# A decoder layer on one Trainium2 core: the second RMSNorm's last squares and powers moved forward, and the first weight splits of the MLP held behind named instructions

## The chip, the cores and the metric

The kernel runs on one core of one Trainium2 chip. The metric is device time in microseconds, the median of three runs of the whole program. A core has a matrix engine (TensorE, in the rows PE, with its weight loads as PEld), a vector engine (VectorE, DVE), an activation engine (ScalarE, ACT), a general engine (GpSimd, POOL) and an engine that issues most of the loads (SyncE, SP). Each works through its own instructions in a fixed order, and they wait for each other by semaphores.

## The reference, cut to what matters

One layer over 256 tokens of width 1024, everything in float32. Three attention mixers and their gates come first and are not touched here. What the change touches is the seam between the end of that part and the gated MLP:

```
x = x + merged @ w_out
h = rmsnorm(x, norm_ffn)                  # x * rsqrt(mean(x*x) + 1e-6) * g, row by row
u = h @ w_up                              # 1024 -> 2 * 2816
u = causal depthwise conv of width 3 over the tokens, + bias
x = x + (silu(u[:, :2816]) * u[:, 2816:]) @ w_down
out = rmsnorm(x, norm_final)
```

## The kernel before

**Products in three parts.** Every float32 operand of a matmul is split into a rounded high part (`hi`, written by ScalarE as fp32r) and the remainder (`lo`, by VectorE). `mm3` then makes three products: lo by hi, hi by lo, hi by hi. A weight unit (`Unit`) is 128 x 2048 numbers, loaded by one DMA of SyncE into a `raw` tile; ScalarE writes `whi` from it in two halves (L223) and VectorE writes `wlo = raw - whi` in two halves (L227). Five units are in flight at a time.

**The middle.** Tokens are in two tiles of 128 (t = 0, 1), channels in two halves of 512 (n = 0, 1). Four sums `acc[t][n]` in PSUM hold the output projection. As each is finished (`flush`), VectorE adds the residual into `xs` (L750, `add(t, n)`), ScalarE squares it and sums the row (L168, `square(t, n)`), and TensorE turns it into channel-major order (L760, `turned`). ScalarE scales the turned blocks by g and writes `hn_hi` (L767), VectorE writes `hn_lo` from the turned block in PSUM and `hn_hi` in SBUF (L770).

**The norm is applied late.** The MLP's first products (unit `fa0`, the first 256 columns of the activated half, and `fu0`, of the other half, into four PSUM tiles `firsts`) are made with x * g, not yet divided by the root mean square. The factor is made on the side: VectorE adds the two half sums of squares and epsilon (`msf`, L177), GpSimd raises them to the power -0.5 (`rsf`, L179), two matmuls against the identity spread them over all partitions (L822), ScalarE copies that to SBUF (`rows`, L823), and VectorE multiplies each product by it (L841 in `conv`).

**Order.** From the first `flush` to the end of the first products, the code says the order on all engines but SyncE (`manual_schedule`). A scheduler places what comes after that (the further units, `fd0`, `fd1`, `fa2`, ...), and may put it between those instructions. On TensorE the middle is: turn, 16 products with `hn_hi` (the first four of eight blocks k), turn, 16 with `hn_lo`, 16 with `hn_hi` (the other four k), 16 with `hn_lo`, the two spreading matmuls, 32 products with `wlo` (L827). Then come the MLP's units: per 128 channels c, 24 products for each half, the convolution (one ScalarE pass L842 and two VectorE passes L844), silu (L861), the product (L863), its split into `fh` (L866) and `fl` (L867), and, one channel block later, 12 products of 512 columns into the output sums (`later`). `fd0` is the first unit of w_down, needed for the first of these.

Of the kernel before, what the change touches and what calls it, by code (L numbers as in the profile page):

```python
# [127 lines left out]
def decoder_layer(ctx: ExitStack, tc, x, small_b, table, w1, wts, norms, out):  # L128
# [77 lines left out]
    class Unit:  # L206
# [17 lines left out]

        def lo(self, i, steps, eng=None):
            sl = slice(self.size * i // steps, self.size * (i + 1) // steps)
            (eng or nc.vector).tensor_sub(self.parts[1][:, sl], self.raw[:, sl], self.parts[0][:, sl].bitcast(F32))  # L227

        def split(self, steps, eng):
            for i in range(steps):  # L230
# [521 lines left out]
    def square(t, n):  # L752
        return square_mean(xs[:, t, HALF[n]], spare[0][:, HALF[n]], f"f{t}{n}")
# [15 lines left out]
    def turn_lo(c):  # L769
        nc.vector.scalar_tensor_tensor(h_lo[:, c, :], xT[c], g_ffn[:, c:c + 1], h_hi[:, c, :].bitcast(F32),  # L770
                                       op0=ALU.mult, op1=ALU.subtract)

    fu = dict(first)
    firsts = [gtile() for _ in range(4)]

    def first_products(part, b, ks):

        for k in ks:
            for i in range(2):
                for j, u in enumerate((fu["fa0"], fu["fu0"])):  # L780
                    nc.tensor.matmul(firsts[2 * i + j], u[part][:, k, i * P:(i + 1) * P], b[:, k, :],
                                     start=b is h_hi and k == 0, stop=False)

    with tc.manual_schedule(engines={mybir.EngineType.Activation, mybir.EngineType.DVE, mybir.EngineType.Pool,
                                     mybir.EngineType.PE}):

        sq = {}
        for t in range(NT):
            flush(t, 0)
            add(t, 0)  # L790
            sq[t, 0] = square(t, 0)
        flush(0, 1)
        add(0, 1)
        xT += turned(0)
        flush(1, 1)

        def split_x(c0):

            for c in (c0, c0 + 1):
                turn_hi(c)  # L800
            for c in (c0, c0 + 1):
                turn_lo(c)
        split_x(0)
        add(1, 1)
        split_x(2)
        first_products(0, h_hi, range(4))
        u_f.lo(0, 2)
        xT += turned(1)
        first_products(0, h_lo, range(4))
        split_x(4)  # L810
        split_x(6)
        first_products(0, h_hi, range(4, KC))
        u_f.lo(1, 2)
        for t in range(NT):
            sq[t, 1] = square(t, 1)
        rs = [rstd_of([sq[t, 0], sq[t, 1]], f"f{t}") for t in range(NT)]
        fu["fa1"] = unit("fa1")
        first_products(0, h_lo, range(4, KC))

        rp = psa.tile([P, 512], F32, name="acc00")[:, :S]  # L820
        for t in range(NT):
            nc.tensor.matmul(rp[:, t * P:(t + 1) * P], rs[t].to_broadcast([P, P]), ident, start=True, stop=True)  # L822
        nc.scalar.activation(rows, rp, AF.Copy)  # L823
        for i in range(4):
            for k in range(KC):
                u = fu[("fa0", "fu0")[i % 2]]
                nc.tensor.matmul(firsts[i], u[1][:, k, i // 2 * P:(i // 2 + 1) * P], h_hi[:, k, :], start=False,  # L827
                                 stop=k == KC - 1)
        fu["fu1"] = unit("fu1")
    waiting.clear()  # L830


    merge.close()
    mpool = ctx.enter_context(tc.tile_pool(name="ffn", bufs=2))
    acc = sums()

    def conv(ps, ch):
        y = mpool.tile([P, S], F32, name="cy", bufs=3)
        u = scaled.pop(0)
        scaled.append(u)  # L840
        nc.vector.tensor_mul(u, ps, rows)  # L841
        nc.scalar.activation(y, u, AF.Identity, bias=vec_c[:, 3, ch:ch + 1], scale=vec_c[:, 2, ch:ch + 1])  # L842
        for w, sh in ((1, 1), (0, 2)):
            nc.vector.scalar_tensor_tensor(y[:, sh:], u[:, :S - sh], vec_c[:, w, ch:ch + 1], y[:, sh:],  # L844
                                           op0=ALU.mult, op1=ALU.add)
        return y

    for i in range(NFF // 2):
        ua, uu, ud = (fu.pop(f"f{w}{i}", None) or unit(f"f{w}{i}", 4 if i == 1 and w != "d" else 2) for w in "aud")
        for c in range(2):  # L850
            ch = 2 * i + c

            def up(u):
                ps = gtile()
                for k in range(KC):
                    mm3(ps, u[0][:, k, c * P:(c + 1) * P], u[1][:, k, c * P:(c + 1) * P],
                        h_hi[:, k, :], h_lo[:, k, :], k == 0, k == KC - 1)
                return ps
            a = conv(firsts[2 * ch] if ch < 2 else up(ua), ch)
            sa = mpool.tile([P, S], F32, name="sa")  # L860
            nc.scalar.activation(sa, a, AF.Silu)  # L861
            b = conv(firsts[2 * ch + 1] if ch < 2 else up(uu), NFF + ch)
            nc.vector.tensor_mul(sa, sa, b)  # L863
            fh = mpool.tile([P, S], F32R, name="fh", bufs=4)
            fl = mpool.tile([P, S], F32R, name="fl", bufs=4)
            nc.scalar.activation(fh, sa, AF.Copy)  # L866
            nc.vector.tensor_sub(fl, sa, fh.bitcast(F32))  # L867
            later(acc, fh, fl, ud, c, ch == 0, ch == NFF - 1, 1 if ch < NFF - 3 else 3)
# [39 lines left out]
```

## Time and profile before

| what | value |
|---|---|
| median of 3 runs | 440.69 us (439.71 to 441.37) |
| the profiled execution | 441.25 us |
| its span, first to last instruction | 439.4 us |
| mean granted TensorE clock, as a share of full speed | 0.991 |
| TensorE busy | 428.6 us, 98% of the span |
| VectorE busy | 307.0 us, 70% |
| ScalarE busy | 241.6 us, 55% |
| GpSimd busy | 16.3 us, 4% |
| loads from HBM | 76.52 MB |

The profiled execution lasts 1.85 us longer than its span, and 0.56 us longer than the median. Busy matmul time is modelled at its ends, so the starts of matmuls say more than their busy time. An engine that is off the path has idle time that costs nothing; what counts is where TensorE, the busiest one, stands still or runs at a lower clock.

### The profile page before, as it was taken

The numbers are of one execution on the slowest core, as the hardware profiler recorded it, in microseconds if no ns is written. First come the engines' busy times: TensorE is split into PE (matmuls) and PEld (weight loads), VectorE is DVE, ScalarE is ACT, GpSimd is POOL, SyncE is SP. The second block draws the span as 40 slices with busy tenths as digits, with TensorE's granted clock in tenths as the row PEclk, the third lists the DMA queues.
The fourth block names the chain that finished last, engine by engine and source line by source line (L and its number), as shares of the span: only waits on it lengthen the run. The fifth ranks groups of instructions, "written<-read, shape, count | busy, mean of one in ns | idle before, by whom it ended". The sixth has DMA issues, their size and how long they took to land.

```text
span 439.4 us, 7725 instructions
## 1 busy us (share of the span) xinstructions
PE 428.6 (98%) x3104; PEld 392.2 (89%) x3104; DVE 307.0 (70%) x637; ACT 241.6 (55%) x421; POOL 16.3 (4%) x19
## 2 busy tenths in 40 slices
PE   8999999999999999999999899999999999999993
PEld 8998877976789998999998799999999999999982
DVE  5666743888465597549355789897797887887854
ACT  6443452458676774455346686465465564574423
POOL 4201000000000000000000300000000000000001
PEclk9999999999999999999999999999999999999998
DMA  8989545431027694544540455752752733700002
GB/s 307 393 321 355 204 157 227 169 119 68 31 101 272 273 367 187 192 151 154 204 164 0 172 213 198 280 205 99 271 188 101 288 147 142 285 3 1 2 0 95
DMA packets 12611, 78.09 MB, mean 178 GB/s; under 512 B 1392, under 2 KB 1408, under 8 KB 4640
## 3 DMA queue, kind: packets, MB, share of 16 engines
q1 hardware_dynamic: 12000, 75.48, 46.2%
q0 software_dynamic: 576, 2.12, 1.5%
q8 instruction: 24, 0.39, 0.4%
q14 instruction: 11, 0.09, 0.1%
HBM read 76.52 MB, written 1.07 MB: 177 GB/s over the span
## 4 chain that ended last, share of the span: by engine, by line
PE 91%; DVE 2%; issue 2%; POOL 2%; DMA 1%; ACT 1%; POOLq 0%; SPq 0%
PE g L241 21%; PE g L239 21%; PE g L240 21%; PE acc L239 6%; PE acc L240 6%; PE acc L241 6%; PE s L443 3%; PE o L475 2%; PE t L454 2%; DMA raw<-in_wts_dram 1%; PE g L827 1%; PE o L537 1%; POOL rsf L179 1%; POOL wlo L227 1%; DVE hn_lo L770 1%
## 5 line engine op out<-in xcount | busy, mean ns | idle before, releaser
L227 DVE TENSOR_TENSOR wlo<-raw,whi 128x1024 fp32r<-128x1024 f32 (+2 forms) x130 | 152.8, 1206 | 51.5 <-ACT whi L223 51.1
L239 PE MATMUL g<-hn_hi,wlo 128*128 128x256 f32 x632 | 180.7, 286 | 0.0
L241 PE MATMUL g<-hn_hi,whi 128*128 128x256 f32 x632 | 179.9, 285 | 0.0
L240 PE MATMUL g<-hn_lo,whi 128*128 128x256 f32 x632 | 179.9, 285 | 0.0
L223 ACT ACTIVATE whi<-raw 128x1024 fp32r<-128x1024 f32 (+2 forms) x130 | 129.6, 1039 | 40.8 <-PE g L241 28.4
L239 PEld LDWEIGHTS g<-hn_hi,wlo 128*128 128x128 f32 x632 | 121.1, 192 | 3.8 <-issue 2.3
L240 PEld LDWEIGHTS g<-hn_lo,whi 128*128 128x128 f32 x632 | 121.1, 192 | 2.7 <-issue 1.9
L241 PEld LDWEIGHTS g<-hn_hi,whi 128*128 128x128 f32 x632 | 121.1, 192 | 1.4 <-issue 1.3
L844 DVE SCALAR_TENSOR_TENSOR cy<-xn,small_b,cy 128x255 f32<-128x255 f32 (+1 forms) x88 | 41.8, 481 | 11.4 <-ACT cy L842 10.4
L842 ACT ACTIVATE cy<-xn,small_b 128x256 f32<-128x256 f32 x44 | 26.0, 596 | 17.2 <-DVE xn L841 17.2
L239 PE MATMUL acc<-whi,fl 128*128 128x512 f32 x88 | 34.5, 392 | 0.0
L240 PE MATMUL acc<-wlo,fh 128*128 128x512 f32 x88 | 34.5, 392 | 0.0
L241 PE MATMUL acc<-whi,fh 128*128 128x512 f32 x88 | 34.2, 389 | 0.0
L866 ACT ACTIVATE fh<-sa 128x256 fp32r<-128x256 f32 x22 | 9.1, 416 | 33.8 <-DVE sa L863 33.8
L841 DVE TENSOR_TENSOR xn<-g,xn 128x256 f32<-128x256 f32 x44 | 18.5, 422 | 13.2 <-PE g L241 9.6
L654 ACT ACTIVATE gl<-g 128x256 f32<-128x256 f32 x24 | 9.1, 381 | 23.9 <-PE g L241 23.9
L241 PEld LDWEIGHTS acc<-whi,fh 128*128 128x128 f32 x88 | 16.5, 188 | 3.6
L239 PEld LDWEIGHTS acc<-whi,fl 128*128 128x128 f32 x88 | 16.6, 189 | 3.0
L240 PEld LDWEIGHTS acc<-wlo,fh 128*128 128x128 f32 x88 | 16.6, 189 | 2.8
L240 PE MATMUL g<-o_lo,whi 128*128 128x256 f32 x64 | 18.1, 283 | 0.0
L241 PE MATMUL g<-o_hi,whi 128*128 128x256 f32 x64 | 18.1, 283 | 0.0
L239 PE MATMUL g<-o_hi,wlo 128*128 128x256 f32 x64 | 18.1, 283 | 0.0
(180 smaller groups left out, 512.9 us busy)
## 6 DMA issues: line engine op xcount, KB each, us to landing
raw<-in_wts_dram SPq DMA_DIRECT2D x62, 1024.0 KB, 4.9
gl<-in_w_dram SPq DMA_DIRECT2D x8, 512.0 KB, 7.3
raw<-in_wts_dram SPq DMA_DIRECT2D x2, 804.0 KB, 7.8
raw<-in_wts_dram SPq DMA_DIRECT2D x3, 512.0 KB, 6.4
T<-tvd POOLq DMA_DIRECT2D x1, 1280.0 KB, 13.2
xs<-in_x_dram SPq DMA_DIRECT2D x2, 516.0 KB, 3.7
out_dram<-raw SPq DMA_DIRECT2D x4, 256.0 KB, 2.2
T<-tvd POOLq DMA_DIRECT2D x1, 768.0 KB, 8.4
```

The lines of the kernel that those rows point to most:

```text
L223: nc.scalar.activation(self.parts[0][:, sl], self.raw[:, sl], AF.Copy)
L227: (eng or nc.vector).tensor_sub(self.parts[1][:, sl], self.raw[:, sl], self.parts[0][:, sl].bitcast(F32))
L239: nc.tensor.matmul(ps, al, bh, start=start, stop=False)
L240: nc.tensor.matmul(ps, ah, bl, start=False, stop=False)
L241: nc.tensor.matmul(ps, ah, bh, start=False, stop=stop)
L443: nc.tensor.matmul(pss[i][:, o], q[rows, q0:q0 + P], k[rows, 0:k1], start=True, stop=True)
L454: nc.tensor.transpose(ps[:, i * P:(i + 1) * P], b, ident)
L654: nc.scalar.activation(gl[c][:, b, :], chunk_T(plain(u, c)), AF.Copy)
L841: nc.vector.tensor_mul(u, ps, rows)
L842: nc.scalar.activation(y, u, AF.Identity, bias=vec_c[:, 3, ch:ch + 1], scale=vec_c[:, 2, ch:ch + 1])
L844: nc.vector.scalar_tensor_tensor(y[:, sh:], u[:, :S - sh], vec_c[:, w, ch:ch + 1], y[:, sh:], op0=ALU.mult, op1=ALU.add)
L866: nc.scalar.activation(fh, sa, AF.Copy)
```

## The change

It reorders the middle and touches no arithmetic. The squares of the second channel half move on ScalarE in front of the second four `hn_hi` blocks, and their `msf` on VectorE behind the fourth `hn_lo` block; the two spreading matmuls move in front of the last 16 `hn_lo` products. The two `lo` halves of `fu0` now stand together behind all eight `hn_lo`. `fa1` and `fu1` are split at places that the code names, `fd0` is held until `rows` and the second `lo` half of `fu1` are done (`issue_after`, which tells the scheduler behind which instruction it may place the work), and the units of the next two channel pairs behind a convolution's ScalarE pass each. The multiplication by `rows` becomes `by_rstd`, called where the product ends.

```diff
         split_x(0)
         add(1, 1)
         split_x(2)
+        for t in range(NT):
+            sq[t, 1] = square(t, 1)
         first_products(0, h_hi, range(4))
-        u_f.lo(0, 2)
+
+        rs = [rstd_of([sq[t, 0], sq[t, 1]], f"f{t}") for t in range(NT)]
         xT += turned(1)
         first_products(0, h_lo, range(4))
         split_x(4)
         split_x(6)
+        for i in range(2):
+            u_f.lo(i, 2)
+        u_n = Unit("fa1")
+        fu["fa1"] = u_n.views
+        for i in range(2):
+            u_n.hi(i, 2)
         first_products(0, h_hi, range(4, KC))
-        u_f.lo(1, 2)
-        for t in range(NT):
-            sq[t, 1] = square(t, 1)
-        rs = [rstd_of([sq[t, 0], sq[t, 1]], f"f{t}") for t in range(NT)]
-        fu["fa1"] = unit("fa1")
-        first_products(0, h_lo, range(4, KC))
 
         rp = psa.tile([P, 512], F32, name="acc00")[:, :S]
         for t in range(NT):
             nc.tensor.matmul(rp[:, t * P:(t + 1) * P], rs[t].to_broadcast([P, P]), ident, start=True, stop=True)
-        nc.scalar.activation(rows, rp, AF.Copy)
+        on_act = [nc.scalar.activation(rows, rp, AF.Copy)]
+        for i in range(2):
+            u_n.lo(i, 2)
+        first_products(0, h_lo, range(4, KC))
+        u_n = Unit("fu1")
+        fu["fu1"] = u_n.views
+        for i in range(2):
+            u_n.hi(i, 2)
         for i in range(4):
             for k in range(KC):
                 u = fu[("fa0", "fu0")[i % 2]]
                 nc.tensor.matmul(firsts[i], u[1][:, k, i // 2 * P:(i // 2 + 1) * P], h_hi[:, k, :], start=False,
                                  stop=k == KC - 1)
-        fu["fu1"] = unit("fu1")
+            if i < 3:
+                firsts[i] = by_rstd(firsts[i])
+            if i < 2:
+                on_dve = u_n.lo(i, 2)
     waiting.clear()
+    with tc.issue_after(on_act[0].ins), tc.issue_after(on_dve.ins):
+        fu["fd0"] = unit("fd0")
...
     for i in range(NFF // 2):
-        ua, uu, ud = (fu.pop(f"f{w}{i}", None) or unit(f"f{w}{i}", 4 if i == 1 and w != "d" else 2) for w in "aud")
+        with tc.issue_after(on_act[3 + i].ins) if i in (1, 2) else ExitStack():
+            ua, uu, ud = [fu.pop(f"f{w}{i}", None) or unit(f"f{w}{i}") for w in "aud"]
```

On TensorE, before, behind the second turning (L760): `rsf` is the power, `g` the four `firsts`, the tile after the last `acc` is the spread factor.

```order
L781 MATMUL g<-hn_hi,whi 128x256 x16
L760 MATMUL acc_2853<-ident,xs 128x128 x4
L760 MATMUL acc_2854<-ident,xs 128x128 x4
L781 MATMUL g<-hn_lo,whi 128x256 x16
L781 MATMUL g<-hn_hi,whi 128x256 x16
L781 MATMUL g<-hn_lo,whi 128x256 x16
L822 MATMUL acc_2940<-ident,rsf_2910 128x128
L822 MATMUL acc_2940<-ident,rsf_2914 128x128
L827 MATMUL g<-hn_hi,wlo 128x256 x32
```

The same place on TensorE in the changed kernel (L787, L831 and L843 are the old L781, L822 and L827):

```order
L787 MATMUL g<-hn_hi,whi 128x256 x16
L760 MATMUL acc_2864<-ident,xs 128x128 x4
L760 MATMUL acc_2865<-ident,xs 128x128 x4
L787 MATMUL g<-hn_lo,whi 128x256 x16
L787 MATMUL g<-hn_hi,whi 128x256 x16
L831 MATMUL acc_2922<-ident,rsf_2858 128x128
L831 MATMUL acc_2922<-ident,rsf_2862 128x128
L787 MATMUL g<-hn_lo,whi 128x256 x16
L843 MATMUL g<-hn_hi,wlo 128x256 x32
```

The two spreading matmuls have moved ahead of 16 products; no row has come or gone.

On VectorE, before, from the residual addition of the last quarter on (`msf` is the mean of squares, `wlo` the lo half of a weight unit, `xn` a product times `rows`):

```order
L750 TENSOR_TENSOR xs<-acc_1949,xs 128x512
L770 SCALAR_TENSOR_TENSOR hn_lo<-acc_2812,xs,hn_hi 128x256 x2
L227 TENSOR_TENSOR wlo<-raw,whi 128x1024 x2
L770 SCALAR_TENSOR_TENSOR hn_lo<-acc_2853,xs,hn_hi 128x256 x2
L770 SCALAR_TENSOR_TENSOR hn_lo<-acc_2854,xs,hn_hi 128x256 x2
L227 TENSOR_TENSOR wlo<-raw,whi 128x1024
L177 TENSOR_SCALAR msf_2908<-ssf_2793,ssf_2904 128x1
L177 TENSOR_SCALAR msf_2912<-ssf_2802,ssf_2906 128x1
L227 TENSOR_TENSOR wlo<-raw,whi 128x1024 x3
L841 TENSOR_TENSOR xn_2779<-g,xn_2779 128x256
L227 TENSOR_TENSOR wlo<-raw,whi 128x1024 x2
```

And in the changed kernel (L776 is the old L841):

```order
L750 TENSOR_TENSOR xs<-acc_1949,xs 128x512
L770 SCALAR_TENSOR_TENSOR hn_lo<-acc_2812,xs,hn_hi 128x256 x2
L177 TENSOR_SCALAR msf_2856<-ssf_2793,ssf_2836 128x1
L177 TENSOR_SCALAR msf_2860<-ssf_2802,ssf_2838 128x1
L770 SCALAR_TENSOR_TENSOR hn_lo<-acc_2864,xs,hn_hi 128x256 x2
L770 SCALAR_TENSOR_TENSOR hn_lo<-acc_2865,xs,hn_hi 128x256 x2
L227 TENSOR_TENSOR wlo<-raw,whi 128x1024 x4
L776 TENSOR_TENSOR xn_2779<-g,xn_2779 128x256
L227 TENSOR_TENSOR wlo<-raw,whi 128x1024
L776 TENSOR_TENSOR xn_2779<-g,xn_2779 128x256
L227 TENSOR_TENSOR wlo<-raw,whi 128x1024
```

The two `msf` stand three weight halves earlier, right in front of four `hn_lo`; behind them four weight halves are in one row.

On ScalarE, before, from the first four `hn_hi` to `rows` (L823); `ssf` are the sums of squares:

```order
L767 ACTIVATE hn_hi<-acc_2811,xs 128x256 x2
L767 ACTIVATE hn_hi<-acc_2812,xs 128x256 x2
L223 ACTIVATE whi<-raw 128x1024 x2
L767 ACTIVATE hn_hi<-acc_2853,xs 128x256 x2
L767 ACTIVATE hn_hi<-acc_2854,xs 128x256 x2
L168 ACTIVATE xn_2778,ssf_2904<-xs 128x512
L168 ACTIVATE xn_2778,ssf_2906<-xs 128x512
L223 ACTIVATE whi<-raw 128x1024 x3
L823 ACTIVATE xn_2779<-acc_2940 128x256
L223 ACTIVATE whi<-raw 128x1024 x2
```

And in the changed kernel (L832 is the old L823, L860 the old L842):

```order
L767 ACTIVATE hn_hi<-acc_2811,xs 128x256 x2
L767 ACTIVATE hn_hi<-acc_2812,xs 128x256 x2
L168 ACTIVATE xn_2778,ssf_2836<-xs 128x512
L168 ACTIVATE xn_2778,ssf_2838<-xs 128x512
L767 ACTIVATE hn_hi<-acc_2864,xs 128x256 x2
L767 ACTIVATE hn_hi<-acc_2865,xs 128x256 x2
L223 ACTIVATE whi<-raw 128x1024 x2
L832 ACTIVATE xn_2779<-acc_2922 128x256
L223 ACTIVATE whi<-raw 128x1024 x4
L860 ACTIVATE cy<-xn_2779,small_b 128x256 x3
```

The squares stand in the place of two halves of a weight unit (`fd0`), and these come behind `rows`.

## Rows read from the trace of the kernel before

**Rows 1.** Page: busy time, share of the span and instructions of each engine.
```profile
PE 428.6 (98%) x3104; PEld 392.2 (89%) x3104; DVE 307.0 (70%) x637; ACT 241.6 (55%) x421; POOL 16.3 (4%) x19
```

**Rows 2.** Chain that ended last, 246 to 257 us: start, us, what.
```profile
246.74 3.87 POOL rsf L179
```

**Rows 3.** Timeline of TensorE: start, us to the last end, line, tiles, count [idle before].
```profile
241.80 1.04 PE L760 MATMUL acc<-ident,xs 128*128 128x128 f32 x8
242.59 2.15 PE L781 MATMUL g<-hn_lo,whi 128*128 128x256 f32 x16
244.58 2.08 PE L781 MATMUL g<-hn_hi,whi 128*128 128x256 f32 x16
246.50 2.08 PE L781 MATMUL g<-hn_lo,whi 128*128 128x256 f32 x16
250.65 1.32 PE L822 MATMUL acc<-ident,rsf 128*128 128x128 f32 x4 [2.07 <-POOL rsf L179]
256.74 0.28 PE L239 MATMUL g<-hn_hi,wlo 128*128 128x256 f32 x1
...
263.34 0.40 PE L239 MATMUL acc<-whi,fl 128*128 128x512 f32 x1
...
282.22 0.40 PE L239 MATMUL acc<-whi,fl 128*128 128x512 f32 x1
```

**Rows 4.** Stretches around the wait: busy time of engines, granted clock, DMA share, GB/s.
```profile
251.00:254.40 3.40, 3.39 (x17) 3.22 (x16) 0.61 (x2) 2.39 (x4) 0.13 (x1) 0.50 1.00 410
254.40:256.70 2.30, 2.30 (x21) 2.30 (x21) 2.30 (x3) 2.30 (x3) 0.00 (x0) 1.00 0.61 246
```

**Rows 5.** Timeline of GpSimd, beginning, middle and end of the program.
```profile
8.81 4.77 POOL L227 TENSOR_TENSOR wlo<-raw,whi 128x1024 fp32r<-128x1024 f32 x2 [1.06 <-ACT whi L306]
...
246.74 4.39 POOL L179 TENSOR_TENSOR rsf<-msf,half 128x1 f32<-128x1 f32 x2 [211.66 <-DVE msf L177]
...
430.09 0.93 POOL L179 TENSOR_TENSOR rsz<-msz,half 128x1 f32<-128x1 f32 x1 [178.96 <-DVE msz L177]
```

**Rows 6.** Timeline of VectorE beside these GpSimd instructions.
```profile
10.80 1.65 DVE L315 SCALAR_TENSOR_TENSOR hn_lo<-t,xs,hn_hi 128x256 fp32r<-128x256 f32 x4
...
246.69 3.50 DVE L227 TENSOR_TENSOR wlo<-raw,whi 128x1024 fp32r<-128x1024 f32 x3
...
429.93 0.68 DVE L877 TENSOR_TENSOR raw<-xs,g 128x512 f32<-128x512 f32 x1
```

**Rows 7.** Timeline of ScalarE: the squares, the `hn_hi` and the silu table.
```profile
238.27 1.57 ACT L767 ACTIVATE hn_hi<-acc,xs 128x256 fp32r<-128x256 f32 x4 [0.30 <-PE acc L760]
...
242.43 1.57 ACT L767 ACTIVATE hn_hi<-acc,xs 128x256 fp32r<-128x256 f32 x4 [0.34 <-PE acc L760]
243.88 0.65 ACT L168 ACTIVATE xn<-xs 128x512 f32<-128x512 f32 x1
244.65 0.63 ACT L168 ACTIVATE xn<-xs 128x512 f32<-128x512 f32 x1
...
257.86 1.28 ACT L861 ACT_TABLE_LOAD   x1
```

**Rows 8.** Timeline of VectorE in the middle and the MLP's first channels.
```profile
240.08 0.69 DVE L750 TENSOR_TENSOR xs<-acc,xs 128x512 f32<-128x512 f32 x1
240.69 0.87 DVE L770 SCALAR_TENSOR_TENSOR hn_lo<-acc,xs,hn_hi 128x256 fp32r<-128x256 f32 x2
...
243.74 1.66 DVE L770 SCALAR_TENSOR_TENSOR hn_lo<-acc,xs,hn_hi 128x256 fp32r<-128x256 f32 x4
...
253.79 0.42 DVE L841 TENSOR_TENSOR xn<-g,xn 128x256 f32<-128x256 f32 x1 [3.61 <-PE g L827]
...
264.19 0.75 DVE L841 TENSOR_TENSOR xn<-g,xn 128x256 f32<-128x256 f32 x2
...
281.04 0.41 DVE L867 TENSOR_TENSOR fl<-sa,fh 128x256 fp32r<-128x256 f32 x1
```

**Rows 9.** Stretch 240.69 to 281.46 us: busy PE, PEld, DVE, ACT, POOL (instructions), clock, DMA, GB/s.
```profile
240.69:281.46 40.77, 38.69 (x277) 36.81 (x276) 35.85 (x62) 27.34 (x43) 4.39 (x2) 0.96 0.59 214
```

More of the change, by code (lines that the diff above doesn't have):

```diff
@@ L226, in lo @@
             sl = slice(self.size * i // steps, self.size * (i + 1) // steps)
-            (eng or nc.vector).tensor_sub(self.parts[1][:, sl], self.raw[:, sl], self.parts[0][:, sl].bitcast(F32))
+            return (eng or nc.vector).tensor_sub(self.parts[1][:, sl], self.raw[:, sl], self.parts[0][:, sl].bitcast(F32))
         def split(self, steps, eng):
@@ L771, in turn_lo, with by_rstd @@
                                        op0=ALU.mult, op1=ALU.subtract)
+    def by_rstd(ps):
+        u = scaled.pop(0)
+        scaled.append(u)
+        nc.vector.tensor_mul(u, ps, rows)
+        return u
     fu = dict(first)
@@ L835, in decoder_layer, with conv @@
     acc = sums()
-    def conv(ps, ch):
+    def conv(u, ch):
         y = mpool.tile([P, S], F32, name="cy", bufs=3)
[L839 to L842, printed above, removed]
+        on_act.append(nc.scalar.activation(y, u, AF.Identity, bias=vec_c[:, 3, ch:ch + 1], scale=vec_c[:, 2, ch:ch + 1]))
         for w, sh in ((1, 1), (0, 2)):
@@ L857, in up @@
                         h_hi[:, k, :], h_lo[:, k, :], k == 0, k == KC - 1)
-                return ps
+                return by_rstd(ps)
             a = conv(firsts[2 * ch] if ch < 2 else up(ua), ch)
@@ L861, in decoder_layer @@
             nc.scalar.activation(sa, a, AF.Silu)
-            b = conv(firsts[2 * ch + 1] if ch < 2 else up(uu), NFF + ch)
+            b = conv(firsts[1] if ch == 0 else by_rstd(firsts[3]) if ch == 1 else up(uu), NFF + ch)
             nc.vector.tensor_mul(sa, sa, b)
```

## The prediction

> **What bounds the kernel now.** I read the page first: TensorE is busy for 98% of the span [rows 1], so a change can only pay where TensorE stands or runs slow. The chain of work that ended last shows the one long piece in it that isn't TensorE's: the first power on GpSimd, 3.87 us from 246.74 [rows 2]. TensorE's timeline shows what that costs [rows 3]. Products of 256 columns start 0.12 us apart when nothing is in the way (16 of them from 244.58 to 246.50). The last 16 `hn_lo` products start at 246.50, so the spreading matmuls could start at 248.42; they start at 250.65, after an idle time that ends with the power. The first MLP product starts at 256.74.
>
> The table of stretches shows a second loss [rows 4]: from 251.00 to 254.40 the granted clock is 0.50, that is 1.2 GHz in place of 2.4, behind an idle time of 2.07 us; from 254.40 on it is 1.00 again. The mean from 240.69 to 281.46 is 0.96 [rows 9], which these 3.4 us account for (1.7 of 40.77), so there is no other fall nearby. 3.4 us at half speed do 1.7 us of work.
>
> Why is the power slow? It begins at 246.74 and the pair of powers takes 4.39 us [rows 5], so the second takes about 0.52: a power by itself is short. VectorE runs three `wlo` subtractions from 246.69 to 250.19 [rows 6], and the first power ends 0.42 us after them (246.74 + 3.87 = 250.61). At the end of the program a power begins at 430.09, under a VectorE product of two SBUF operands that runs from 429.93 to 430.61, and ends at 431.02, 0.41 us after it. Two cases, one pattern: the power gets through only when the VectorE subtraction or product is over, and a run without a gap holds it for the whole run. The opposite case is there too: while GpSimd subtracted `wlo` from 8.81 to 13.58 [rows 5], VectorE's `hn_lo` form, whose first operand is in PSUM, took 1.65 us for four [rows 6], as in the middle, where GpSimd was idle (1.66) [rows 8]. That form doesn't collide.
>
> **The change, part by part.** *Powers.* ScalarE ends its first four `hn_hi` at 239.84 (238.27 + 1.57), and squares follow each other by 0.77 us [rows 7]. The first moved square runs from 239.84 to 240.6; the second needs the last residual addition, which ends at 240.77 [rows 8], and ends at about 241.55. VectorE is through its fourth `hn_lo` at 241.56, makes `msf` and then has nothing to do until the next `hn_hi` pair is there, at 242.43 + 0.8 = 243.25 [rows 7]. So the powers run from about 241.75, 0.5 each, to 242.85. Even without that pause the four `hn_lo` that follow don't hold them; the first subtraction of SBUF operands comes behind these, at 243.25 + 1.66 = 244.9. The powers have 3.15 us for 1.1. TensorE asks for them at 246.50.
>
> The Trainium skill ("SBUF — State Buffer", Who interferes with whom) gives this its rule: a VectorE instruction with two SBUF inputs and a GpSimd instruction that reads SBUF exclude each other for a whole instruction, and one with at most one SBUF input doesn't contend. The trace agrees with the second half (1.65 against 1.66 us, above); of the first half it shows more than the rule says, a hold over three instructions.
>
> *TensorE.* From 246.50 to 256.74 it now spends 10.24 us. The same instructions without wait and at full clock: 48 products of 0.12 are 5.76, and the four records of the spreading matmuls at the pace of the eight turning matmuls (241.80 to 242.59, 0.10 each) are 0.40; together 6.16. **Gain 4.08 us**, the MLP starting at 252.66. It is made of 2.23 of waiting (250.65 less 248.42) and 1.85 of slow clock and of the second power (6.09 us from 250.65 to 256.74, against 4.24). The wait alone, with the clock still falling, is the lower bound, 2.2; if the spreading matmuls keep the 0.33 us each that their row allows (1.32 / 4), the gain is 3.2. I take 4.08: nothing stands in front of them to cool the engine.
>
> *What moves on ScalarE.* The squares go in front of the second four `hn_hi`, which wait for the turning until 242.43 anyway; the squares are done at 241.55. Cover 0.9 us, cost nothing; were it gone, the first of these `hn_hi` would be late, and TensorE asks for it at 244.58, 1.7 us after it is written. The two `fd0` halves that stood there go behind `rows`.
>
> *What moves on VectorE.* Two `fd0` halves at 1.14 us each ((3.50 - 1.22) / 2, taking 1.22 for one alone) leave the middle and stand behind the three `rows` products, in front of the first convolution. That is the part that may cost. VectorE's account to the point where the second `later` step starts (its operand `fl`, of the third channel block, ends at 281.45 [rows 8]): from 240.69 it is busy for 35.85 us [rows 9]. The changed order up to the same `fl` has the same rows but one convolution pass (0.40) less: 35.45. It must stand still for the pause above (241.8 to 243.25, 1.45), until the first of `firsts` is complete (four weight halves end at 249.45; the eighth `wlo` product starts at 248.82 + 0.84 and ends 0.28 later, 249.94: 0.5), and for some 0.3 in short chains. 240.69 + 35.45 + 2.3 = 278.45. TensorE wants it at 282.22 - 4.08, and three products (0.36) later than before, because the order has them in front: 278.50. Nothing to spare. The first `later` step is as tight: TensorE reaches it at 263.34 - 4.08 + 9 x 0.12 = 260.34. On the other side `rows` times the first product starts at 250.0; three such products (0.34 behind another, from 0.75 for two [rows 8]), four weight halves and three convolution passes end at 256.85; table load 1.28 [rows 7], silu, product, `fh` and `fl` at about 0.42 each, with two VectorE instructions between: 260.3. Before, these two had 0.8 us or more, because TensorE was late. A delay at the first is shared by the second, so I charge one of them: between 0 and 1 us, taken as **0.3**, since both sums come out within 0.05 of the due time and bare starts leave out some handovers.
>
> *Loads.* SyncE issues the same loads in the same order. The raw tile of `fu0` comes free at about 247.3 (244.9 + 1.14 + 1.22), and the load of `fa2` waits for it; ScalarE reaches that split only behind the first two `fh`, after 260: more than 12 us of cover. The changed order holds no instruction more or less.
>
> **Sum.** 4.08 - 0.3 = 3.8 us off the span of the profiled execution: 435.6, and 437.45 for its time of 441.25. That execution lay 0.56 above the median; off the median of 440.69 it is **436.9 us**.
>
> **Rivals.** *Late operands (the stall moves into the MLP).* VectorE is busy for 35.85 of 40.77 us here and gets 4 us less; if handovers cost it 1.0 us more than I counted, TensorE waits 1 us at a `later` step, and if such a wait is enough for the clock to fall again, 1.7 more go: 440.69 - 4.08 + 2.7 = 439.3. For it: two due times without a margin. Against it: VectorE has kept its back-to-back pace through the stretch before, with under 1.4 us of idle time beside the 3.61 at 253.79. It decides from 0.3 us of lateness on.
>
> *The powers are caught again (slower).* If one isn't through at 244.9, it waits for the run of four weight halves, until 244.9 + 3 x 1.14 + 1.22 = 249.5, and ends at 249.9; the second, at 250.4. TensorE now stands there with 16 products more behind the wait: 250.45 + 0.2 + 5.76, and 1.7 for the clock, is 258.1, 1.4 later than now: 442.1. It needs 2 us of delay between `msf` and the powers that no row shows.
>
> By the skill's rule, a hold of one instruction, such a power would slip in behind the first weight half; TensorE would then wait for about 1 us, which is 438 us; of the chance of this rival I give it a quarter.
>
> *The clock falls all the same.* If 1.2 GHz was granted for another reason than the idle time, 1.7 of the gain is missing: 438.6. Against it: the rows have 1.00 just before and after.
>
> **How the numbers follow.** The forecast, 436.0 to 438.0, has 0.70; late operands 0.15; powers caught 0.08; the clock 0.05; something slower that I don't see 0.02. About 0.5% (2.2 us) is what a measurement of this kernel can tell from no change, so "faster" means under 438.5. Faster: the forecast, half of the late operands and half of the clock's, 0.80; the same: the rest of these and most of the caught powers, 0.16; slower: 0.04. The forecast alone leaves out 3 in 10, so the range goes up into the late operands, to 439.0, and down to 435.7, which is the full 4.08 and 0.9 more, about what the fastest run lies under the median (0.98).
>
> **What would show it.** Powers of about 0.5 us each near 242, the spreading matmuls right behind 16 `hn_hi` products without idle time, a clock of 1.00 through 246 to 260, the first MLP product 6.2 us after the last 16 `hn_hi` products. Right or wrong on the cost: idle time of TensorE at the first two `later` steps, under 0.5 us in all. The prediction is wrong if a power takes over 2 us, or if TensorE idles more than 1 us between 252 and 280.

## The result, and the profile after

| | before | changed |
|---|---|---|
| median of 5 runs | 440.69 us (439.71 to 441.39) | 438.12 us (437.23 to 438.27) |
| profiled execution, its span | 441.25, 439.4 us | 438.12, 436.3 us |
| mean granted TensorE clock in it | 0.991 | 0.994 |

The ratio is 0.9927, with a 95% interval of 0.9913 to 0.9942: faster by 2.6 us, 0.7%. The page's first line, which answers to [rows 1]:

```profile
PE 426.7 (98%) x3104; PEld 390.5 (89%) x3104; DVE 306.9 (70%) x637; ACT 240.8 (55%) x421; POOL 12.9 (3%) x19
```

GpSimd is busy for 3.4 us less with as many instructions. TensorE's timeline, as in [rows 3] (start, us to the last end, line, tiles, count, idle time before):

```profile
240.66 2.08 PE L787 MATMUL g<-hn_hi,whi 128*128 128x256 f32 x16
...
245.35 2.08 PE L787 MATMUL g<-hn_hi,whi 128*128 128x256 f32 x16
247.27 0.60 PE L831 MATMUL acc<-ident,rsf 128*128 128x128 f32 x4
247.63 2.16 PE L787 MATMUL g<-hn_lo,whi 128*128 128x256 f32 x16
249.63 4.00 PE L843 MATMUL g<-hn_hi,wlo 128*128 128x256 f32 x32
...
253.47 0.28 PE L239 MATMUL g<-hn_hi,wlo 128*128 128x256 f32 x1
...
261.26 0.47 PE L239 MATMUL acc<-whi,fl 128*128 128x512 f32 x1
```

No idle time stands at the spreading matmuls (L831). From the end of the second 16 `hn_hi` products to the first MLP product it is 6.20 us (247.27 to 253.47), where it was 10.24 us before (246.50 to 256.74). The 32 `wlo` products start 0.12 us apart throughout. GpSimd and VectorE, as in [rows 5] and [rows 8]:

```profile
242.54 1.08 POOL L179 TENSOR_TENSOR rsf<-msf,half 128x1 f32<-128x1 f32 x2 [206.31 <-DVE msf L177]
```

```profile
242.25 0.37 DVE L177 TENSOR_SCALAR msf<-ssf,ssf 128x1 f32<-128x1 f32 x2
244.08 1.66 DVE L770 SCALAR_TENSOR_TENSOR hn_lo<-acc,xs,hn_hi 128x256 fp32r<-128x256 f32 x4 [1.46 <-ACT hn_hi L767]
245.66 4.62 DVE L227 TENSOR_TENSOR wlo<-raw,whi 128x1024 fp32r<-128x1024 f32 x4
...
260.70 0.42 DVE L886 TENSOR_TENSOR fl<-sa,fh 128x256 fp32r<-128x256 f32 x1
```

The pair of powers takes 1.08 us where it took 4.39, and lies in VectorE's pause of 1.46 us. The table of stretches, against [rows 4] (busy PE, PEld, DVE, ACT, POOL with instructions, granted clock, DMA share, GB/s):

```profile
246.00:250.00 4.00, 4.00 (x36) 4.00 (x36) 4.00 (x4) 2.76 (x4) 0.00 (x0) 1.00 0.21 47
250.00:255.00 5.00, 5.00 (x44) 5.00 (x43) 4.42 (x7) 3.79 (x6) 0.00 (x0) 1.00 0.95 374
```

The clock stays at 1.00 here. One thing was not foreseen: this execution is 0.78 us late before anything that the change touches. The first `hn_hi` products of the middle start at 240.66, before at 239.88, and the lateness begins with the first weight load. ScalarE's first split of it in the changed kernel, and then in the kernel before:

```profile
8.81 0.63 ACT L306 ACTIVATE whi<-raw 128x512 fp32r<-128x512 f32 x1 [0.97 <-DMA raw<-in_wts_dram]
```

```profile
8.10 0.63 ACT L306 ACTIVATE whi<-raw 128x512 fp32r<-128x512 f32 x1 [0.31 <-DMA raw<-in_wts_dram]
```

So I cut each span in three. **Start**: until the first 16 `hn_hi` products of the middle. **Seam**: from there to the first MLP product. **Rest**: from there to the end. Each is the difference of two starts on TensorE's timeline, or of a start and the span; spans are given to 0.1 us, so a rest is good to 0.05. Before: 239.88 + 16.86 + 182.66. Changed: 240.66 + 12.81 + 182.83. The change gave 4.05 in the seam and cost 0.17 in the rest; the start took 0.78 back.

### The profile page after: what moved, and what is told of

It is laid out like the page before. It is cut to its first block, busy times and chain, and to the rows that moved or that the text cites. A ratio compares the mean times of both kernels' runs of the same rounds, so it can differ in the third digit from the quotient of the medians.

```text
span 436.3 us, 7726 instructions
## 1 busy us (share of the span) xinstructions
PE 426.7 (98%) x3104; PEld 390.5 (89%) x3104; DVE 306.9 (70%) x637; ACT 240.8 (55%) x421; POOL 12.9 (3%) x19
## 3 DMA queue, kind: packets, MB, share of 16 engines
q0 software_dynamic: 576, 2.12, 1.4%
## 4 chain that ended last, share of the span: by engine, by line
PE 93%; DMA 2%; issue 1%; POOL 1%; DVE 1%; ACT 1%; POOLq 0%; SPq 0%
PE g L241 21%; PE g L239 21%; PE g L240 21%; PE acc L239 6%; PE acc L240 6%; PE acc L241 6%; PE s L443 3%; PE o L475 2%; PE t L454 2%; PE g L787 2%; DMA raw<-in_wts_dram 2%; PE o L537 1%; PE g L843 1%; POOL wlo L227 1%; PE acc L760 0%
## 5 line engine op out<-in xcount | busy, mean ns | idle before, releaser
L860 ACT ACTIVATE cy<-xn,small_b 128x256 f32<-128x256 f32 x44 | 26.1, 594 | 17.2 <-DVE xn L776 17.2
L776 DVE TENSOR_TENSOR xn<-g,xn 128x256 f32<-128x256 f32 x44 | 18.5, 420 | 9.6 <-PE g L241 9.0
```

Of the source, the lines that this page charges most:

```text
L860: on_act.append(nc.scalar.activation(y, u, AF.Identity, bias=vec_c[:, 3, ch:ch + 1], scale=vec_c[:, 2, ch:ch + 1]))
```

## The experiments

The theory: the gain is the power alone, set free from the run of two-operand subtractions; what follows is TensorE's wait and the slow clock behind it. Rivals: the spreading matmuls' new place or the gates carry part of it, and a power is held for one instruction at most. Open were also the 0.78 us at the start, and why the median moved by 2.6 us where the seam and the rest gave 3.9. All twelve runs in one table; the three parts are of the profiled execution, the clocks are the lowest and highest mean granted clock of the timed executions. The kernel before, run beside them, had a median of 440.60 us beside no_gates, spread_last, vector_loaded and power_free_at_end, and of 441.39 beside the others.

| run | median us | ratio to before, 95% | start | seam | rest | clocks |
|---|---|---|---|---|---|---|
| before_again | 441.50 | 0.9991 to 1.0022 | 240.59 | 15.45 | 182.66 | 0.991 to 0.996 |
| after_again | 437.44 | 0.9900 to 0.9939 | 239.70 | 12.81 | 182.89 | 0.995 to 0.998 |
| early_alone | 437.95 | 0.9904 to 0.9936 | 239.78 | 12.81 | 182.81 | 0.995 to 0.998 |
| powers_late | 443.67 | 1.0036 to 1.0073 | 240.56 | 18.45 | 182.89 | 0.987 to 0.994 |
| run_broken | 438.53 | 0.9918 to 0.9950 | 240.58 | 13.53 | 182.69 | 0.996 to 0.998 |
| run_broken_later | 439.35 | 0.9946 to 0.9978 | 240.14 | 14.67 | 182.69 | 0.994 to 0.998 |
| no_gates | 437.44 | 0.9903 to 0.9948 | 239.83 | 12.81 | 182.76 | 0.995 to 0.998 |
| spread_last | 437.70 | 0.9907 to 0.9949 | 240.00 | 12.81 | 182.89 | 0.995 to 0.998 |
| vector_loaded | 437.50 | 0.9903 to 0.9947 | 239.96 | 12.81 | 182.83 | 0.994 to 0.997 |
| power_free_at_end | 438.31 | 0.9925 to 0.9973 | 239.85 | 12.81 | 183.34 | 0.994 to 0.997 |
| end_swapped | 437.22 | 0.9898 to 0.9941 | 241.60 | 12.81 | 182.69 | 0.995 to 0.997 |
| free_and_end | 437.18 | 0.9894 to 0.9933 | 239.98 | 12.82 | 182.60 | 0.994 to 0.997 |

### One part alone: the powers early

The kernel before with this edit:

```diff
         split_x(2)
+        for t in range(NT):
+            sq[t, 1] = square(t, 1)
         first_products(0, h_hi, range(4))
         u_f.lo(0, 2)
+        rs = [rstd_of([sq[t, 0], sq[t, 1]], f"f{t}") for t in range(NT)]
         xT += turned(1)
...
         u_f.lo(1, 2)
-        for t in range(NT):
-            sq[t, 1] = square(t, 1)
-        rs = [rstd_of([sq[t, 0], sq[t, 1]], f"f{t}") for t in range(NT)]
```

> The kernel before, with one part of the change alone: the two last squares and the powers move forward, while the spreading matmuls stay behind all 48 products, nothing is gated and the scheduler may put fd0 into the middle again. Theory (the gain is the power, set free from the run of subtractions): no power over 1.7 us (at most one subtraction in its way), no idle time at the spreading matmuls, clock 1.00 from 246 to 260, the seam from the last 16 hn_hi-type products to the first MLP product 4.0 us shorter than in the kernel before; time 3.0 to 4.1 us under the kernel before, about that of the changed kernel or below it. Rival (the place of the spreading matmuls or the gates carry the gain): less than 1.5 us under the kernel before.

Measured: 437.95 us against 441.39 beside it, the whole gain, with the seam of the changed kernel to the hundredth. VectorE, GpSimd and TensorE of this run:

```profile
242.74 1.22 DVE L227 TENSOR_TENSOR wlo<-raw,whi 128x1024 fp32r<-128x1024 f32 x1
```

```profile
242.79 2.11 POOL L179 TENSOR_TENSOR rsf<-msf,half 128x1 f32<-128x1 f32 x2 [205.82 <-DVE msf L177]
```

```profile
248.31 0.60 PE L822 MATMUL acc<-ident,rsf 128*128 128x128 f32 x4
```

One subtraction did catch the first power, which cost 1.0 us that nobody waited for. The move of squares and powers gives the whole gain; the rival falls.

### That part undone: the powers late

The changed kernel with this edit:

```diff
-        rs = [rstd_of([sq[t, 0], sq[t, 1]], f"f{t}") for t in range(NT)]
         xT += turned(1)
...
         split_x(6)
+        rs = [rstd_of([sq[t, 0], sq[t, 1]], f"f{t}") for t in range(NT)]
         for i in range(2):
             u_f.lo(i, 2)
```

> The changed kernel with one part undone: the mean of squares and the powers stand right ahead of the run of four weight halves again; squares, spreading matmuls and gates stay as changed. Theory (a run without a gap holds the power to its end): the first power ends 0.4 us behind the fourth subtraction and takes 4.5 to 5 us; TensorE stands for 3.9 us at the spreading matmuls, then 3.4 us at half clock; 5.5 us over the changed kernel, 443.6, slower than the kernel before. Rival one (a power is held for one instruction only): the powers take about 1.5 us each, TensorE waits 1.7 us, 438.6 to 440.8. Rival two (the powers were never what mattered, the rest of the change is): 438.1.

Measured: 443.67, slower than the kernel before. The chain of this run (start, us, what), VectorE's run of subtractions, TensorE, and the stretch behind the wait:

```profile
245.85 5.00 POOL rsf L179
```

```profile
245.80 4.63 DVE L227 TENSOR_TENSOR wlo<-raw,whi 128x1024 fp32r<-128x1024 f32 x4
```

```profile
250.90 1.32 PE L831 MATMUL acc<-ident,rsf 128*128 128x128 f32 x4 [3.57 <-POOL rsf L179]
251.87 3.47 PE L787 MATMUL g<-hn_lo,whi 128*128 128x256 f32 x16
```

```profile
251.00:254.40 3.40, 3.36 (x16) 3.17 (x17) 0.00 (x0) 2.14 (x3) 0.37 (x1) 0.56 0.99 405
```

The first power ends 0.42 us behind the fourth subtraction (250.85 against 250.43), and TensorE, after 3.57 us of idle time, does 16 products in 3.31 us (251.87 to 255.18) instead of 2.0. Squares, gates and spreading matmuls stand as in the changed kernel, and none of them helps.

### The run broken, after one subtraction and after two

powers_late with this edit:

```diff
-        for i in range(2):
-            u_f.lo(i, 2)
+        u_f.lo(0, 2)
+        for c in (5, 6, 7):
+            nc.vector.scalar_tensor_tensor(spare[0][:, c % 2 * S:(c % 2 + 1) * S], xT[c], g_ffn[:, c:c + 1],
+                                           h_hi[:, c, :].bitcast(F32), op0=ALU.mult, op1=ALU.subtract)
+        u_f.lo(1, 2)
```

In the second kernel both `lo` halves stand ahead of the added instructions.

> As the run before it in this list (powers late), but three more VectorE instructions of the hn_lo form, whose first operand is in PSUM, stand behind the first of the four subtractions; they write a tile that nothing reads. Theory (what holds a power is the two operands in SBUF, instruction by instruction in a row, and it gets through as soon as the row has a break): the first power takes about 1.6 us, ends 0.4 us behind the first subtraction, the second takes 0.5 under the added instructions; TensorE stands for 0.8 to 1.0 us at the spreading matmuls, and VectorE's added 1.2 us come back as a wait of about 0.5 at the first later step: 439.0 to 440.0, so more work on VectorE makes it 4 us faster than with the run unbroken. Rival (the power waits until VectorE has no more work queued): it ends behind the fourth subtraction, 445.

> As the run with the broken row of subtractions, but the three added instructions stand behind the second subtraction instead of the first. Theory (a row holds the power to its end, whatever its length): the first power ends 0.4 us behind the second subtraction, 2.7 us after it began, the second takes 0.5; TensorE loses 1.4 us before the spreading matmuls and 0.4 between them. If the clock stays at 1.00 behind an idle time of 1.3 us: 439.5 to 440.1. If it falls as behind 2.07 us in the kernel before's first profile: 441.0 to 441.8. Rival (one instruction at most is held): the power takes 1.6 us, 438.5 as with the earlier break.

Measured: 438.53 and 439.35. VectorE and GpSimd with the break behind the first subtraction (L823 are the added instructions):

```profile
245.82 1.22 DVE L227 TENSOR_TENSOR wlo<-raw,whi 128x1024 fp32r<-128x1024 f32 x1
246.96 1.26 DVE L823 SCALAR_TENSOR_TENSOR xn<-acc,xs,hn_hi 128x256 f32<-128x256 f32 x3
248.13 3.49 DVE L227 TENSOR_TENSOR wlo<-raw,whi 128x1024 fp32r<-128x1024 f32 x3
```

```profile
245.87 2.12 POOL L179 TENSOR_TENSOR rsf<-msf,half 128x1 f32<-128x1 f32 x2 [210.04 <-DVE msf L177]
```

With the break behind the second: VectorE's row, the chain, TensorE and the stretch behind the wait:

```profile
245.38 2.35 DVE L227 TENSOR_TENSOR wlo<-raw,whi 128x1024 fp32r<-128x1024 f32 x2
```

```profile
245.43 2.73 POOL rsf L179
```

```profile
248.21 1.02 PE L834 MATMUL acc<-ident,rsf 128*128 128x128 f32 x4 [1.29 <-POOL rsf L179]
```

```profile
251.00:254.40 3.40, 3.40 (x31) 3.40 (x30) 2.38 (x5) 3.19 (x5) 0.00 (x0) 1.00 0.86 318
```

The first power takes 1.58 us (of the 2.12; the second, under the added instructions, takes 0.55), 2.73, 3.87 [rows 2] and 5.00 us behind rows of one, two, three and four subtractions: about 1.14 us more for each. More work on VectorE made the program 5 us faster than powers_late, because it was of the form that lets a power through. Behind 1.29 us of idle time the clock stayed at 1.00 in the profile; the mean clocks of the other executions (0.994 to 0.998) show no sign of a fall either. Both came out under what I had written, by 0.5 and 0.2 us, and that is mostly the rest: the first `later` step did not wait for VectorE's added 1.2 us. In both kernels it starts 8.88 us after the first MLP product, behind 74 products of the next channels; in the changed kernel it is 7.79 us and 64 products. The scheduler had moved it.

### Gates, spreading matmuls, VectorE's load

The changed kernel without its gates:

```diff
-    with tc.issue_after(on_act[0].ins), tc.issue_after(on_dve.ins):
-        fu["fd0"] = unit("fd0")
+    fu["fd0"] = unit("fd0")
...
-        with tc.issue_after(on_act[3 + i].ins) if i in (1, 2) else ExitStack():
+        with ExitStack():
```

The changed kernel with the spreading matmuls last:

```diff
         first_products(0, h_hi, range(4, KC))
-        rp = psa.tile([P, 512], F32, name="acc00")[:, :S]
-        for t in range(NT):
-            nc.tensor.matmul(rp[:, t * P:(t + 1) * P], rs[t].to_broadcast([P, P]), ident, start=True, stop=True)
-        on_act = [nc.scalar.activation(rows, rp, AF.Copy)]
         for i in range(2):
             u_n.lo(i, 2)
         first_products(0, h_lo, range(4, KC))
+        rp = psa.tile([P, 512], F32, name="acc00")[:, :S]
...
```

And the changed kernel with one more subtraction on VectorE:

```diff
                 on_dve = u_n.lo(i, 2)
+            if i == 2:
+                nc.vector.tensor_sub(spare[0], xs[:, 0, :D], xs[:, 1, :D])
```

> The changed kernel without its gates: fd0 and the units of the second and third channel pair may be placed wherever the scheduler likes, and fd0's first halves are back between the two squares on ScalarE and in the middle's order. Theory (the gain is the power alone, the gates carry nothing): powers under 0.7 us each, no idle time at the spreading matmuls, under 0.5 us of it at the first two later steps, 437.5 to 438.5. Rival (without the gates the weight halves stand in the way of the squares or of the first later step): 439 or more, with the wait visible at one of these.

> The changed kernel with the spreading matmuls back behind all 48 products, powers early. Theory: the powers are long done and rows are still written before the first product is whole, so nothing changes: 437.5 to 438.5, same seam within 0.2 us. Rival (their earlier place carries part of the gain, since rows comes later and the first multiplications by it, and so the first later step, with it): TensorE waits 1 us or more at the first later step, 439.0 to 439.5.

> The changed kernel with one more VectorE subtraction of 128x1024 (both operands in SBUF, 1.14 us) in front of fd0's two lo halves; it writes a tile that nothing reads. It measures the margin of VectorE up to the first later step, where the changed kernel waits 0.18 us. Theory (VectorE has no margin left there): nearly all of it comes back as TensorE's wait there, 1.1 to 1.4 us in all, 439.0 to 439.6, and more if the clock falls behind it. Rival (the 0.18 is a handover and VectorE has slack): under 0.4 us of wait, 438.0 to 438.4.

Measured: 437.44, 437.70 and 437.50, all with the seam of 12.81 and a rest within 0.07 us of the changed kernel's. By the medians, gates and the new place of the spreading matmuls carry nothing that can be measured. TensorE's starts are given to 0.01 us and show a little more. From the first MLP product to the last product of the program it is 175.19 and 175.18 us in the two profiles of the kernel before, 175.37 and 175.38 in those of the changed kernel, 175.38 in spread_last, but 175.21 in no_gates. There the first `later` step stands behind 75 products and waits for nothing. So the changed kernel's cost of 0.19 us in the MLP hangs on where the step stands: early_alone, without gates and with the step behind 55 products, pays 0.15 (175.33).

The third run didn't test what it was made for. The added subtraction and the first later step in it:

```profile
253.44 1.22 DVE L850 TENSOR_TENSOR xn<-xs 128x1024 f32<-128x1024 f32 x1
```

```profile
261.70 0.47 PE L239 MATMUL acc<-whi,fl 128*128 128x512 f32 x1
```

The step starts 8.93 us after the first MLP product (252.77), where it started after 7.79 in the changed kernel: 1.14 later, since 74 products of the next channels stand in front of it instead of 64. It is 0.05 us, and its second product 0.08 us, behind a pace without gaps. The scheduler, which places what comes behind the hand-written order, moved the step. So neither theory nor rival was tried as I had put it: VectorE's margin at a fixed place of the step is still unknown, and this delay, which the scheduler knew of, cost nothing.

### The starts and the clock: both kernels again

> The kernel before, once more with a profile. The changed kernel's profile was 0.78 us late before the middle, with the first weight load landing 0.71 us later, though the program is the same up to there. Theory (the landing of the first load varies from run to run): the landing of this run differs from 6.43 us after its issue by some tenths, and the span goes with it one for one; the time is 439.7 to 441.4. Rival (the late landing belongs to the changed program): 6.43 again within 0.1, and a span of 439.4.

> The changed kernel once more, with a profile, beside the two that follow. Theory (the landing of the first load is one of two levels near 6.4 and 7.1 us, by run, and the clock does not fall in the middle in any run): span 435.5 with the early landing, 436.3 with the late one, all mean clocks 0.994 or above, median 437.3 to 438.3. Rival (something in the changed program delays the first load): late again.

TensorE in the second execution of the kernel before, and its stretch as in [rows 4]:

```profile
247.20 2.08 PE L781 MATMUL g<-hn_lo,whi 128*128 128x256 f32 x16
251.35 1.02 PE L822 MATMUL acc<-ident,rsf 128*128 128x128 f32 x4 [2.07 <-POOL rsf L179]
252.13 4.07 PE L827 MATMUL g<-hn_hi,wlo 128*128 128x256 f32 x32
```

```profile
251.00:254.40 3.40, 3.00 (x23) 2.81 (x24) 0.97 (x2) 1.99 (x3) 0.83 (x2) 1.00 1.00 414
```

The same idle time, 2.07 us, and this time the clock did not fall: a seam of 15.45 in place of 16.86. The execution started 0.71 us later and ended 0.7 us earlier. The span doesn't follow the landing (the arrival of the first weight load) alone, as both of my expectations had it. Of 58 executions of the kernel before that ran beside these kernels, 34 have a mean clock of 0.991 to 0.993 and a median of 441.86 us, and 24 have 0.995 or 0.996 and 440.19; none lies between. In 54 executions of the eight kernels with early powers, the changed one included, none is below 0.994. I read the two groups as executions with and without the fall behind the wait. That is argued: there is one profile of each kind (mean clocks 0.991 and 0.996), and the mean also holds the slow clock of the program's last microseconds, when the products are over (0.50 from 432 us on in the changed kernel's first profile, from 436 on in that of the kernel before).

The landing varies too, whatever the kernel: ScalarE's first weight split starts between 7.74 us (the changed kernel, second profile) and 9.29 (end_swapped) in the fourteen profiles, and the middle starts 231.7 to 232.3 us behind that, at 239.70 to 241.60. It isn't the changed program that was late. What sets the landing was not tried.

### The same remedy at the program's end

In end_swapped the scaling behind the last power becomes, for the last 128 tokens (`r` is that power):

```diff
         for n in range(2):
...
-            nc.vector.tensor_mul(y[:, t, sl], xs[:, t, sl], gfin[:, sl])
+            if t == 0 or n == 0:
+                nc.vector.tensor_mul(y[:, t, sl], xs[:, t, sl], gfin[:, sl])
...
-            if n == 0:
+            if t == 1 and n == 1:
+                nc.vector.scalar_tensor_tensor(y[:, t, sl], xs[:, t, sl], r, gfin[:, sl], op0=ALU.mult, op1=ALU.mult)
+            elif n == t:
                 nc.vector.tensor_scalar_mul(y[:, t, sl], y[:, t, sl], r)
             else:
                 nc.scalar.activation(y[:, t, sl], y[:, t, sl], AF.Copy, scale=r)
```

power_free_at_end, tried first, has the two halves the other way round. free_and_end is no_gates with the edit above.

> The changed kernel with the same remedy used at the end of the program: for the last 128 tokens VectorE's product of the second half with g stands in front of the mean of squares and that of the first half is joined with the scaling behind the power, so that no two-operand VectorE instruction runs beside the last power (0.93 us in the changed kernel). Theory: this power takes 0.5 to 0.55 us, the last ScalarE scaling starts 0.4 us earlier after the last residual addition, and the span is 0.3 to 0.5 us shorter for the same landing of the first load: 437.7, at the edge of what 5 rounds tell. Rival (the end is bound by the joined instruction or the stores): within 0.1 us of the changed kernel.

> The remedy at the program's end once more, with the halves exchanged: VectorE's product of the first half stands in front of the last mean of squares, ScalarE scales that half, and the second half is made by one joined VectorE instruction behind the power, so that nothing waits for the tile that the last square writes. Theory: the last power starts 0.3 us behind msz's start as in the changed kernel and takes 0.55 in place of 0.93 us; the end comes 0.35 us earlier, 0.3 to 0.4 off the span at the same landing. Rival: no change within 0.1 us.

> Both that came out at or under the changed kernel: no gates, and the end as in the run before this. Theory (the two are independent: 0.2 us at the first later step, 0.35 at the end): 0.5 us under the changed kernel run beside it at the same landing, 437.0 to 437.6, spans 434.8 to 435.0 with the early landing. Rival (the order that the scheduler finds differs, and the differences between these kernels are no more than run to run): within 0.2 us of it.

Measured: 438.31, 437.22 and 437.18 (437.44 for the changed kernel beside the last two). `msz` is the mean of squares and `rsz` the power of the final norm. GpSimd's last power in the changed kernel, and VectorE and GpSimd in the first attempt:

```profile
431.04 0.93 POOL L179 TENSOR_TENSOR rsz<-msz,half 128x1 f32<-128x1 f32 x1 [3.11 <-DVE msz L177]
```

```profile
429.95 0.69 DVE L903 TENSOR_TENSOR raw<-xs,g 128x512 f32<-128x512 f32 x1 [0.79 <-ACT raw L168]
```

```profile
430.85 0.55 POOL L179 TENSOR_TENSOR rsz<-msz,half 128x1 f32<-128x1 f32 x1 [3.71 <-DVE msz L177]
```

The power is short now, 0.55 us, but the product ahead of it had to wait for the last square, which writes its squares into the same tile: the rest is 0.5 us longer. With the halves exchanged nothing waits there; VectorE's last instruction then starts 0.87 us behind `msz`, in place of 1.25:

```profile
432.56 0.75 DVE L901 SCALAR_TENSOR_TENSOR raw<-xs,rsz,g 128x512 f32<-128x512 f32 x1 [0.66 <-POOL rsz L179]
```

SyncE's issues of the four output stores, in the changed kernel and in end_swapped:

```profile
428.48 4.84 SPq L903 DMA_DIRECT2D out_dram<-raw  x4
429.42 4.70 SPq L906 DMA_DIRECT2D out_dram<-raw  x4
```

The last one ends 2.57 us behind the start of `msz` in the changed kernel (433.32 less 430.75) and 2.43 in end_swapped (434.12 less 431.69): 0.14 of the 0.38 us gets through. That agrees with the rest, 0.20 shorter than in the changed kernel beside it, within what the spans tell; the 0.29 of free_and_end holds the 0.16 that no_gates saves in the MLP too. Both halves are now done at the same moment, and their stores are issued by one engine one behind the other; that this takes the difference is argued, not shown. By the medians neither is to be told from the changed kernel.

## Why the prediction was right

**Powers.** Forecast from 241.75 to 242.85. Measured 242.54 to 243.62 in an execution that was 0.78 late: 241.76 to 242.84. The reason, a hold by the whole run, is shown by four lengths of it. The Trainium skill ("SBUF — State Buffer", Who interferes with whom) has the shared ports held for one instruction. Here powers_late and both broken runs show that a row of subtractions without a gap holds a power to its end; the measurement decides. By the Trainium skill (the same section) an instruction with at most one SBUF input doesn't contend. That agrees: the second power took 0.55 us under the added instructions, which read one operand from PSUM. The prediction's 0.52 for a power by itself is the difference of two rows; the trace has 0.54 to 0.55.

**TensorE.** Forecast 6.16 us for the 48 products and the spreading matmuls, measured 6.20; gain 4.08, measured 4.05.

**ScalarE, loads.** The cover of 0.9 us for the moved squares is there as 0.84 us of ScalarE's idle time ahead of the second four `hn_hi`, and TensorE waits for no load in the seam.

**VectorE.** Charged 0.3 us, measured 0.17 in the rest, 0.19 between TensorE's starts. `fl` was forecast to end at 260.3; it ended at 261.12, 260.34 without the late start. The first later step starts 0.10 us, and its second product 0.08 us, behind a pace without gaps. The price was near, the reason for the range (0 to 1, and 439.3 for late operands) was not. Where a step stands is the scheduler's choice: vector_loaded shows it moving the step by 1.14 us for nothing, and no_gates a place without a wait.

**The sum.** Forecast span 435.6 for an execution that starts as the profiled one did: 239.88 + 12.81 + 182.83 = 435.5.

**The median, where the working failed.** The step "that execution lay 0.56 above the median; off the median of 440.69 it is 436.9" took one gain for all executions. The profiles show two. With the fall of the clock, as in the profile that I worked from, seam and rest give 4.05 - 0.17 = 3.9; without it, as in the second profile of before, 15.45 - 12.81 - 0.17 = 2.5. The three runs shown lie 1.66 us apart, about the distance of the two groups of 58 (441.86 and 440.19); I read it as noise. The start, 0.8 us apart in the two profiles compared, adds to it. How much of the missing 1.2 us (3.8 forecast, 2.6 measured) is the one and how much the other isn't shown, since the clocks of the five executions of the kernel before aren't on record. With more executions on both sides (median 441.39 for the 58 of before, 437.95 for 11 of the changed kernel) the difference is 3.4, between the two gains. The result of 438.12 lies near the 438.6 that I gave to "the clock falls all the same", but not for that reason: the clock falls in the middle in no profile of the changed kernel, and what varied was the kernel before. That it lies inside the range is in part luck too: the range went up to 439.0 for late operands, and operands were not late.

## What to carry to other kernels

Look for a short GpSimd instruction beside a row of VectorE instructions with two SBUF operands: it lasts as long as what is left of the row, so move it, or break the row with a form that reads PSUM, before touching anything on the engine that waits. Before a gain is taken off a median, ask whether the profiled execution is of the median's kind: cut the spans into parts, and look at the mean clock of every run for signs that one profile doesn't speak for all. An added load on an engine whose work a scheduler orders may move the consumer instead of stalling it, so such a test has to hold the order.

## What the runs showed of the hardware

- The same program with the same idle time of 2.07 us ran on at a clock of 1.00 in one profile and at 0.50, 1.2 GHz, for 3.4 us in another; read from the mean clocks, which is argued, the second happened in 34 of 58 executions. It was worth 1.4 us in the seam. After 1.29 us of idle time (one profile) it stayed at 1.00; after 3.57 (one profile) it was 0.50 from 252 to 254 us, 0.56 over the stretch of the same bounds.
- A power on GpSimd alone takes 0.54 us, and 1.58, 2.73, 3.87 and 5.00 us behind rows of one to four subtractions of 128x1024; it ends 0.41 to 0.42 us behind the row's last one. Under instructions with one operand in PSUM it takes 0.55.
- ScalarE's first split of a weight starts between 7.7 and 9.3 us into the span, in kernels whose program is the same up to there.
